# A hybrid block on one core: scans and branch operands spread over the rotations, operands behind copies, alternating halves, and the last residual in its PSUM bank

## The chip, the cores and the metric

One core of a Trainium2 chip. The time is device microseconds of one execution; before the change the median of three runs is 1061.51 us (1061.37 to 1062.74).

## The reference

One block of a network on 512 tokens behind 16 learned ones (T = 528), width 1024, all in fp32:

```python
z = rms_norm(h) @ w_in
u_rnn, u_gate, q, k, v, g_ret, ga, gb = split(z)
xr = causal_dwconv(u_rnn)                       # 4 taps, 1280 channels
hr = rg_lru(xr)                                 # h_t = a_t h_{t-1} + b_t, 10 blocks of 128 channels
o_a = hr * gelu(u_gate)
q, k = rotary(q, pos), rotary(k, pos) * RET_DK ** -0.5     # 4 heads of 256
o_b = head_rms(retention(q, k, v)) * silu(g_ret)
h = h + (sigmoid(ga) * (o_a @ w_brnn) + sigmoid(gb) * (o_b @ w_bret)) @ w_out
gate, val = split(causal_dwconv(rms_norm(h) @ w_up))
h = h + (gelu(gate) * val) @ w_down
out = rms_norm(h)[:, N_META:]
```

In the scan a = exp(log_a) and b = sqrt(1 - a^2) * (i * x), with two gates r and i that are products of 128 x 128 blocks.

## The kernel before

**Products.** TensorE (PE) works in fp16 on numbers split into a high and a low part: `split` (L93) makes the high part on ScalarE (ACT, L94) and the low part on VectorE (DVE, L95). A product of two such numbers takes three matmuls (`SPLIT`). Weights come from memory in units of 1 MB at most, through SyncE's queue into three buffers (`raw`), and are split into tiles named `wt`, two for a unit, ten buffers in all. The function `tick` issues the next steps of this splitting between the products, as far ahead as the buffers go, and `get` issues what a product needs at once. For some units the weights are also added in pairs on DVE first (L262 to L264), which saves products later.

**`project` (L427 to L433)** computes one tile of 128 channels by all tokens: 8 blocks k of the input, three matmuls for each, for each of two halves of the tokens (264 to 266 columns), 48 matmuls. Half 0 goes into the first and half 1 into the second bank of a PSUM tile of two banks. Blocks k = 0 to 3 use the first `wt` tile of the unit and k = 4 to 7 the second. Half 0 is done in full before half 1 begins.

**The order of work.** Up to `order.close()` each engine works in the order in which the program is written. From there on a scheduler orders the instructions of each engine, by when their inputs can be there and by how long what follows them is. The stages are, with the time at which they run:

- To 80 us: ten blocks n of the recurrent branch. `conv_product` (L629) calls `project` (for n = 0 to 2 half of it is done earlier), `conv_taps` adds four taps, `rnn_gates` makes the two gates.
- 80 to 140 us: ten blocks of the gate branch (L729 to L742, `project` and a gelu). Between them the list `SPREAD` puts steps of the recurrence: tanh, exp, and `rnn_scan` (L676) for blocks 0 to 4 at n = 7 and for blocks 5 to 9 at n = 9. `rnn_scan` is a square root on ACT (L678), a product (L679) and the scan (L680) on DVE, the scan over 528 columns.
- 140 to 230 us: four heads, q and k of each: eight calls of `rotary` (L758), "rotations" below. A rotation runs two `project` products into two PSUM tiles `pp`, then on DVE two cosine products (L770), two sine products (L771) and two sums (L772), and splits the two results (`qk`). Both PSUM tiles are read by both output halves. Four such tiles exist, so a product of the rotation after next waits until the DVE has read a tile of this one. `branch_a` (L745) makes the first branch's operand `oa` for a block: a product with the gate (L747) and a split. Two blocks stand behind rotation 0, three behind rotation 1, two behind 2 and three behind 3.
- 230 to 520 us: scores and values, `retention_out`, and the gates of the retention and of the mix. These run as `fast_products` (L872), seven products of half the size of a tile's, with a PSUM bank `pa` that is used again and again: `keep` (L885 to L887) copies it out on ACT, into `kept` or `last`, with high priority, and the next product waits for the copy. `ob_forms` (L1073) makes the operands of the second branch, 32 splits named `ob` on either engine, and puts them in the list `pending`; `flush` (L1108) issues one of them. `behind_copy` (L287) makes what is issued under it follow the latest `keep` copy, but only while `gating` is set, and it is cleared before the mix.
- 520 to 1000 us: the second branch, the output product, the norm, the feed-forward part.
- The end: the last sixth of the down projection for half of the columns is done by `down_plain` (L1602), 12 matmuls for each of four tiles of 128 tokens. For each tile (L1695 to L1713) DVE adds the residual `hv` (L1702) into `hu`, ACT squares it with a sum (L1704), DVE multiplies with the final gain (L1705), ACT takes the root (L1707), DVE inverts it (L1709) and scales the first 512 columns (L1710), which SyncE stores (L1711), and ACT scales the other 512 (L1712), which are stored on SyncE's or, for the last tile, on ACT's queue (L1713). `weigh` (L1673) has applied the gain to the columns that were ready before.

Of the kernel before, what the change touches and what calls it, by code (L numbers as in the profile page):

```python
# [8 lines left out]
F32 = mybir.dt.float32  # L9
# [5 lines left out]
P = 128  # L15
# [38 lines left out]
def hybrid_block_kernel(ctx, tc, x, meta, norm_mix_g, w_in, conv_w, conv_b, rg_a_w, rg_a_b,  # L54
# [372 lines left out]

    def project(ps, w, col, src, halves, nk):

        for hf, (c0, n) in enumerate(halves):  # L430
            for k in range(nk):
                for aw, ax in SPLIT:
                    nc.tensor.matmul(half_of(ps, halves, hf), w(aw, k, col, P), src(ax, k, c0, n),  # L433
                                     start=k == 0 and (aw, ax) == (0, 0), stop=k == nk - 1 and aw == 1)
# [197 lines left out]
    def conv_product(n):  # L632
        u, col = u_ur[n]
        if n in early:
            ps = early.pop(n)
            project_half(ps, get(u), col, xf, HR, 1)
        else:
            ps = acc("ps")
            project(ps, get(u), col, xf, HR, KD)
        return ps  # L640
# [28 lines left out]
    def rnn_decay(n):  # L669
# [4 lines left out]
        nc.vector.scalar_tensor_tensor(t, a2, 1.0, t, op0=ALU.add, op1=ALU.mult)  # L674

    def rnn_scan(n):  # L676
        r, t, xr = part(half_r, n), part(half_t, n), part(half_x, n)
        nc.scalar.activation(t, t, AF.Sqrt)  # L678
        nc.vector.tensor_mul(t, t, xr)  # L679
        nc.vector.tensor_tensor_scan(xr, r, t, 0.0, op0=ALU.mult, op1=ALU.add)  # L680
# [46 lines left out]
    ahead[0] = 6  # L727
    SPREAD = ((rnn_tanh, 2, 0), (rnn_decay, 3, 0), (rnn_tanh, 4, 5), (rnn_decay, 5, 5), (rnn_scan, 7, 0), (rnn_scan, 9, 5))
    for n in range(NR):  # L729
# [28 lines left out]
    def rotary(u, dst, halves, n, c0, s):  # L758
# [15 lines left out]
        for m in range(2):  # L774
            split(dst[m][:, 0, :n], dst[m][:, 1, :n], turned[m][:, :n], s)

    for h in range(HEADS):
        t = [[piece([P, 2, T], F16, f"qk{h}{i}{m}") for m in range(2)] for i in range(2)]
        qk.append(t)
        rotary(u_q[h], t[0], HQ, TQ, T0, S_QK / (SW * S_XN))  # L780
        if h < 2:
            for n in range(5 * h, 5 * h + 2):
                branch_a(n)
        rotary(u_k[h], t[1], HT, T, 0, S_QK / 16.0 / (SW * S_XN))
        if h < 2:
            for n in range(5 * h + 2, 5 * h + 5):
                branch_a(n)

# [319 lines left out]
    def flush(n=1):  # L1108

        for _ in range(min(n, len(pending))):  # L1110
            with behind_copy():
                pending.pop(0)()
# [488 lines left out]

    def down_plain(pc, tt):  # L1602

        w = wviews[u_dn[11]]
        n = 0
        for half in range(2):
            for b in range(2):
                t, c0 = acts[10 + b]["A%d%d" % (tt // 2 + 1, half + 1)]
                for ax, aw in SPLIT:
                    nc.tensor.matmul(pc, t[:, ax, c0 + tt % 2 * P:c0 + tt % 2 * P + P], w(aw, 2 * half + b, 0, 512),  # L1610
                                     start=n == 0, stop=n == 11)
                    n += 1
# [54 lines left out]
    for tt in range(4):  # L1667
# [3 lines left out]
                             AF.Square, accum_out=sums[:, tt, 0:1])  # L1671

    def weigh(tt, c0):  # L1673
        v = h2[tt].rearrange("p (a b) -> p a b", a=2)[:, :, c0:c0 + 256]
        nc.vector.tensor_tensor(v, v, gfin.rearrange("p (a b) -> p a b", a=2)[:, :, c0:c0 + 256], op=ALU.mult)

    for tt in range(4):
        weigh(tt, 0)
        nc.vector.tensor_scalar(sums[:, tt, 1:2], sums[:, tt, 0:1], inv_d, EPS, op0=ALU.mult, op1=ALU.add)


# [13 lines left out]
    for nm, tt in (("spare", 2), ("P1", 3), ("P6", 0), ("P7", 1)):  # L1695
        down_plain(pd[nm], tt)
        pv = pd[nm].rearrange("p (a b) -> p a b", a=2)
        hv = h2[tt].rearrange("p (a b) -> p a b", a=2)[:, :, 256:512]
        gv = gfin.rearrange("p (a b) -> p a b", a=2)[:, :, 256:512]
        hu = work.tile([P, 512], F32, name="hu", tag="w")  # L1700
        huv = hu.rearrange("p (a b) -> p a b", a=2)
        nc.vector.scalar_tensor_tensor(huv, pv, un, hv, op0=ALU.mult, op1=ALU.add)  # L1702
        junk = work.tile([P, 512], F32, name="junk", tag="w")
        nc.scalar.activation(junk, hu, AF.Square, accum_out=sums[:, tt, 2:3])  # L1704
        nc.vector.tensor_tensor(hv, huv, gv, op=ALU.mult)  # L1705
        sd = small.tile([P, 1], F32, name="sd")
        nc.scalar.activation(sd, sums[:, tt, 2:3], AF.Sqrt, scale=inv_d, bias=sums[:, tt, 1:2])  # L1707
        rs = small.tile([P, 1], F32, name="rs")
        nc.vector.reciprocal(rs, sd)  # L1709
        nc.vector.tensor_scalar_mul(h2[tt][:, 0:512], h2[tt][:, 0:512], rs)  # L1710
        nc.sync.dma_start(o2[tt * P:(tt + 1) * P, 0:512], h2[tt][:, 0:512])  # L1711
        nc.scalar.activation(h2[tt][:, 512:1024], h2[tt][:, 512:1024], AF.Copy, scale=rs)  # L1712
        (nc.scalar if tt == 1 else nc.sync).dma_start(o2[tt * P:(tt + 1) * P, 512:1024], h2[tt][:, 512:1024])  # L1713
    psum["scope"].close()
# [47 lines left out]
```

## Time and profile before

| | |
|---|---|
| median of 3 runs | 1061.51 us (1061.37 to 1062.74) |
| the profiled execution | 1061.5 us, its span 1059.8 us |
| busy in the span | PE 1039.7, DVE 872.8, ACT 594.0, weight load 865.9 us |
| granted TensorE clock | 0.999 |
| moved by DMA | 111.52 MB, of that 2.10 MB written |

The span is the time from the first to the last instruction or transfer that the profile shows; the execution's time has 1.7 us more. In a row of a timeline stand the start, the time taken, the engine, the line, the operation and its tiles (output <- input), and in brackets how long the engine was idle before it and which instruction it waited for. An engine's next instruction starts some 0.1 us before the end that a row shows, since instructions overlap in the engine's pipe: from start to start is the time that it takes up. "PE ps L433 <- DVE t L770" in a list of waits reads: the matmuls of L433 that write tile `ps` waited for the DVE instruction of L770 that writes `t`.

### The profile page before, as it was taken

The page shows a single profiled execution, that of the slowest core. Times are in us where ns is not written, and L with a number is a line of the kernel's source. Part 1 is how long each engine was busy: PE and PEld are TensorE (multiplying, and loading weights), DVE is VectorE, ACT ScalarE, POOL GpSimd, SP SyncE. Part 2 cuts the span into 40 slices and gives each one's busy share as a digit, 9 for nine tenths or more (in the row PEclk, how much of TensorE's full clock was granted, in tenths as well). Part 3 has the DMA queues.
Part 4 walks back from the last instruction along what each step waited for, and adds up shares of the span by engine and source line. Part 5 has one row for each costly group of instructions (what it writes and reads, how often), then busy time and mean ns, then how long its engine had stood idle before and what let it go on. Part 6 is the DMA issues. An engine that isn't in the chain of part 4 may idle for free.

```text
span 1059.8 us, 21437 instructions
## 1 busy us (share of the span) xinstructions
PE 1039.7 (98%) x9187; PEld 865.9 (82%) x9187; DVE 872.8 (82%) x1328; ACT 594.0 (56%) x941; POOL 6.9 (1%) x20
## 2 busy tenths in 40 slices
PE   9999999999999999999999999999999999999997
PEld 6888887875588888888888886588888888888885
DVE  6885699988669999996787885479989898988975
ACT  7568973434356768665454453375555455554442
POOL 2000000000000000000000000000000000000000
PEclk9999999999999999999999999999999999999999
DMA  9231243431012132344334356032423324214312
GB/s 295 97 127 58 81 140 120 159 123 40 1 41 93 68 105 66 107 114 128 108 113 129 98 219 194 1 116 85 160 87 113 120 81 136 65 61 139 101 41 80
DMA packets 109056, 111.52 MB, mean 105 GB/s; under 512 B 5675, under 2 KB 100625, under 8 KB 108961
## 3 DMA queue, kind: packets, MB, share of 16 engines
q1 hardware_dynamic: 108512, 109.74, 32.5%
q8 instruction: 72, 1.18, 0.5%
q10 hardware_dynamic: 160, 0.27, 0.1%
q0 software_dynamic: 288, 0.14, 0.1%
q14 instruction: 24, 0.19, 0.1%
HBM read 108.04 MB, written 2.10 MB: 104 GB/s over the span
## 4 chain that ended last, share of the span: by engine, by line
PE 72%; DVE 16%; ACT 9%; issue 2%; DMA 0%; ACTq 0%; DVEq 0%
PE ps L433 25%; PE P L1598 10%; PE pa L881 9%; DVE wt L95 5%; PE ps L1315 4%; PE pe L881 4%; PE pm L433 4%; PE ps L945 4%; ACT wt L94 2%; PE pb L881 2%; PE pa L1485 2%; PE ps L1035 2%; PE ps L447 2%; DVE rnn L680 1%; PE pa L969 1%
## 5 line engine op out<-in xcount | busy, mean ns | idle before, releaser
L433 PEld LDWEIGHTS <-wt 128*128 128x128 f16 x3840 | 372.5, 97 | 56.0 <-DVE t L770 2.6
L95 DVE SCALAR_TENSOR_TENSOR wt<-raw,wt 128x1024 f16<-128x1024 f32 (+2 forms) x286 | 310.0, 1100 | 57.1 <-ACT wt L94 56.2
L94 ACT ACTIVATE wt<-raw 128x1024 f16<-128x1024 f32 (+2 forms) x286 | 268.2, 958 | 118.7 <-PE P L1598 25.6
L881 PEld LDWEIGHTS <-wt 128*128 128x128 f16 x2016 | 195.2, 97 | 33.5 <-issue 6.7
L433 PE MATMUL ps<-x2h,wt 128*128 128x258 f16 (+1 forms) x1184 | 196.2, 272 | 0.0
L433 PE MATMUL ps<-xh,wt 128*128 128x258 f16 (+4 forms) x1056 | 179.0, 274 | 3.7 <-DVE t L770 2.9
L433 PE MATMUL ps<-x2l,wt 128*128 128x256 f16 (+1 forms) x592 | 160.9, 272 | 0.0
L433 PE MATMUL ps<-xl,wt 128*128 128x256 f16 (+4 forms) x528 | 144.5, 274 | 0.0
L1598 PE MATMUL P<-wt,act 128*128 128x256 f16 x792 | 88.3, 273 | 0.0
L1598 PEld LDWEIGHTS <-act 128*128 128x128 f16 x792 | 77.5, 98 | 9.0
L881 PE MATMUL pa<-xs,wt 128*128 128x258 f16 x576 | 71.3, 273 | 3.0 <-ACT kept L887 2.6
L1463 DVE SCALAR_TENSOR_TENSOR cv<-ps,vt,cv 128x512 f32<-128x512 f32 x80 | 59.3, 745 | 9.1 <-ACT cv L1461 8.5
L433 PE MATMUL pm<-oa,wt 128*128 128x256 f16 (+1 forms) x480 | 54.1, 273 | 0.0
L262 DVE TENSOR_TENSOR raw<-raw 128x1024 f32<-128x1024 f32 x43 | 52.4, 1219 | 0.7
L881 PE MATMUL pa<-ob,wt 128*128 128x257 f16 x384 | 45.7, 274 | 0.6 <-ACT last L887 0.5
L1315 PE MATMUL ps<-wt,mx 128*128 128x512 f16 x192 | 44.3, 378 | 0.0
L945 PE MATMUL ps<-wt,xh 128*128 128x512 f16 x128 | 38.3, 379 | 0.6 <-ACT qk L94 0.5
L1461 ACT ACTIVATE cv<-ps,vt,vt 128x512 f32<-128x512 f32 x40 | 30.5, 766 | 11.9 <-PE ps L433 11.9
L1485 PEld LDWEIGHTS <-wt 128*128 128x128 f16 x336 | 32.6, 97 | 4.4
L94 ACT ACTIVATE qk<-t 128x514 f16<-128x514 f32 (+1 forms) x16 | 10.2, 638 | 40.9 <-DVE t L772 40.9
L1315 PEld LDWEIGHTS <-mx 128*128 128x128 f16 x192 | 17.6, 98 | 18.5
L447 PEld LDWEIGHTS <-wt 128*128 128x128 f16 x288 | 27.9, 97 | 5.0 <-issue 0.6
(319 smaller groups left out, 1503.3 us busy)
## 6 DMA issues: line engine op xcount, KB each, us to landing
raw<-in_w_in SPq DMA_DIRECT2D x36, 1024.0 KB, 5.0
raw<-in_w_up SPq DMA_DIRECT2D x24, 1024.0 KB, 5.2
raw<-in_w_down SPq DMA_DIRECT2D x48, 256.0 KB, 3.4
raw<-in_w_branch_ret SPq DMA_DIRECT2D x16, 512.0 KB, 4.8
raw<-in_w_in SPq DMA_DIRECT2D x12, 512.0 KB, 4.6
raw<-in_w_branch_rnn SPq DMA_DIRECT2D x8, 640.0 KB, 4.7
raw<-in_w_out SPq DMA_DIRECT2D x4, 1024.0 KB, 5.0
xin<-in_x SPq DMA_DIRECT2D x4, 512.0 KB, 5.6
```

The costliest lines, as they stand in the source:

```text
L94: a = nc.scalar.activation(hi, src, AF.Copy, scale=s)
L95: b = nc.vector.scalar_tensor_tensor(lo, src, s, hi, op0=ALU.mult, op1=ALU.subtract)
L262: nc.vector.tensor_tensor(pair, pair, rv[:, :, right].rearrange("p (h k) c -> p h k c", h=2), op=ALU.add)
L433: nc.tensor.matmul(half_of(ps, halves, hf), w(aw, k, col, P), src(ax, k, c0, n), start=k == 0 and (aw, ax) == (0, 0), stop=k == nk - 1 and ...
L447: mm = nc.tensor.matmul(half_of(ps, halves, hf), w(aw, k, col, P), src(ax, k, c0, n), start=k == 0 and (aw, ax) == (0, 0), stop=k == KD - ...
L881: nc.tensor.matmul(ps[:, :n], ws[k // 4](wf, aw, k % 4), src(xf_, ax, k), start=first and k == 0 and (aw, ax) == (0, 0), stop=k == last_k ...
L945: nc.tensor.matmul(pb, xf(ax, k, XF + j0, nb), w(aw, k % 4, 0, 512), start=i == 0, stop=i == 23)
L1315: nc.tensor.matmul(ps[:, n], mx[k][:, a, c0:c0 + P], wo[k // 2](aw, k % 2, n * 512, 512), start=k == 0 and (a, aw) == (0, 0), stop=k == ks ...
L1461: nc.scalar.activation(vv_, taps[2], AF.Identity, scale=vt2[:, 96 + ch:97 + ch], bias=bias)
L1463: nc.vector.scalar_tensor_tensor(vv_, taps[j], vt2[:, 48 * j + ch:48 * j + ch + 1], vv_, op0=ALU.mult, op1=ALU.add)
L1485: nc.tensor.matmul(ps[:, :258], w(wf, aw, k), x2_form(xf_, ax, k), start=first and k == 0 and (aw, ax) == (0, 0), stop=k == 3 and aw == 1, ...
L1598: nc.tensor.matmul(pd[:, 256 * tt:256 * tt + 256], t[:, ax, c0 + tt * P:c0 + tt * P + P], w(wf, aw, i), start=q % 6 == 0 and tt == 0 and i ...
```

## The change

There are four edits. Line numbers behind the first edit move on by 1 to 24: in the rows below, L680 becomes L683, L770 to L772 become L773 to L775, L747 becomes L750, L887 becomes L892 and L920 becomes L925.

1. `project` gets `turns`: for the blocks n < 6 that run it whole (3, 4 and 5), both halves take their turn for each k and each of the three matmuls.
2. The square root is split off from `rnn_scan` and stays where both stood (`rnn_root`). The scans of blocks 5 to 9 go behind rotations 0 to 4, one each. The branch operands of blocks 0 to 4 go behind rotations 0 to 4, one each, and the others behind rotations 5 (two), 6 (two) and 7 (one).
3. `flush` puts the splits of the second branch's operands behind the latest `keep` copy always, and no longer only while `gating` is set.
4. For the last tile ACT writes the residual, scaled, into the PSUM bank ahead of the matmuls, and `down_plain` adds onto it. The square is taken from the bank, the scale and the gain are applied by one DVE instruction, and the two stores take columns 256 to 511 and 0 to 255 of both halves, one on SyncE's and one on ACT's queue, in runs of 1 KB where they were 2 KB. `weigh` becomes an instruction with a scale, and a small one adjusts the sum.

```diff
-    def project(ps, w, col, src, halves, nk):
-
-        for hf, (c0, n) in enumerate(halves):
-            for k in range(nk):
-                for aw, ax in SPLIT:
+    def project(ps, w, col, src, halves, nk, turns=False):
+
+        both = [0, 1]
+        for hfs in [both] if turns else [[0], [1]]:
+            for k, (aw, ax), hf in [(k, s, hf) for k in range(nk) for s in SPLIT for hf in hfs]:
+                    c0, n = halves[hf]
...
-            project(ps, get(u), col, xf, HR, KD)
+            project(ps, get(u), col, xf, HR, KD, n < 6)
...
+    def rnn_root(n):
+        nc.scalar.activation(half_t[n], half_t[n], AF.Sqrt)
+
     def rnn_scan(n):
         r, t, xr = part(half_r, n), part(half_t, n), part(half_x, n)
-        nc.scalar.activation(t, t, AF.Sqrt)
...
-    SPREAD = ((rnn_tanh, 2, 0), (rnn_decay, 3, 0), (rnn_tanh, 4, 5), (rnn_decay, 5, 5), (rnn_scan, 7, 0), (rnn_scan, 9, 5))
+    SPREAD = ((rnn_tanh, 2, 0), (rnn_decay, 3, 0), (rnn_tanh, 4, 5), (rnn_decay, 5, 5), (rnn_root, 7, 0), (rnn_scan, 7, 0), (rnn_root, 9, 5))
...
+    def between(i):
+        if i < 5:
+            rnn_scan(5 + i)
+        for n in ((i,), (5, 6), (7, 8), (9,))[max(0, i - 4)]:
+            branch_a(n)
+
...
         rotary(u_q[h], t[0], HQ, TQ, T0, S_QK / (SW * S_XN))
-        if h < 2:
-            for n in range(5 * h, 5 * h + 2):
-                branch_a(n)
+        between(2 * h)
         rotary(u_k[h], t[1], HT, T, 0, S_QK / 16.0 / (SW * S_XN))
-        if h < 2:
-            for n in range(5 * h + 2, 5 * h + 5):
-                branch_a(n)
+        between(2 * h + 1)
...
-            with behind_copy():
+            with tc.issue_after(last_keep[0]):
                 pending.pop(0)()
...
     def weigh(tt, c0):
...
-        nc.vector.tensor_tensor(v, v, gfin.rearrange("p (a b) -> p a b", a=2)[:, :, c0:c0 + 256], op=ALU.mult)
+        nc.vector.scalar_tensor_tensor(v, v, 1.0 / un if tt == LAST else 1.0,
...
+        if tt == LAST:
+            nc.scalar.activation(pv, hv, AF.Copy, scale=1.0 / un)
+            down_plain(pd[nm], tt, True)
+            junk = work.tile([P, 512], F32, name="junk", tag="w")
+            nc.scalar.activation(junk, pd[nm], AF.Square, scale=un, accum_out=sums[:, tt, 2:3])
+            nc.scalar.activation(sd, sums[:, tt, 2:3], AF.Sqrt, scale=inv_d / (un * un), bias=sums[:, tt, 3:4])
+            nc.vector.reciprocal(rs, sd)
+            ob_ = o2[tt * P:(tt + 1) * P].rearrange("t (a b) -> t a b", a=2)
+            nc.vector.scalar_tensor_tensor(hv, pv, rs, gv, op0=ALU.mult, op1=ALU.mult)
+            nc.sync.dma_start(ob_[:, :, 256:512], hv)
+            nc.scalar.activation(hb[:, :, 0:256], hb[:, :, 0:256], AF.Copy, scale=rs)
+            nc.scalar.dma_start(ob_[:, :, 0:256], hb[:, :, 0:256])
+            break
```

What this does to the order. On DVE, around rotation 0 in the program before, the twelve rows up to the second cosine product (`rnn` are tiles of the recurrence, L679 and L680 its product and scan, `ps` the PSUM tiles, `t_1966` and `t_1971` the two results of the rotation):

```order
L680 SCALAR_TENSOR_TENSOR rnn<-rnn 128x528
L679 TENSOR_TENSOR rnn<-rnn 128x528
L95 SCALAR_TENSOR_TENSOR wt<-raw,wt 128x1024
L680 SCALAR_TENSOR_TENSOR rnn<-rnn 128x528
L679 TENSOR_TENSOR rnn<-rnn 128x528
L95 SCALAR_TENSOR_TENSOR wt<-raw,wt 128x1024
L680 SCALAR_TENSOR_TENSOR rnn<-rnn 128x528
L679 TENSOR_TENSOR rnn<-rnn 128x528
L771 TENSOR_TENSOR t_1967<-ps,rope_1853 128x514
L680 SCALAR_TENSOR_TENSOR rnn<-rnn 128x528
L772 TENSOR_TENSOR t_1966<-t_1966,t_1967 128x514
L770 TENSOR_TENSOR t_1971<-ps,rope_1852 128x514
```

The same place in the changed program (L683 is the scan, L682 its product, `t_1956` and `t_1961` the results):

```order
L95 SCALAR_TENSOR_TENSOR wt<-raw,wt 128x1024
L773 TENSOR_TENSOR t_1956<-ps,rope_1842 128x514
L683 SCALAR_TENSOR_TENSOR rnn<-rnn 128x528
L95 SCALAR_TENSOR_TENSOR wt<-raw,wt 128x1024
L682 TENSOR_TENSOR rnn<-rnn 128x528 x2
L683 SCALAR_TENSOR_TENSOR rnn<-rnn 128x528
L95 SCALAR_TENSOR_TENSOR wt<-raw,wt 128x1024 x2
L774 TENSOR_TENSOR t_1957<-ps,rope_1843 128x514
L773 TENSOR_TENSOR t_1961<-ps,rope_1842 128x514
```

Both programs have the same instructions up to the product of the fifth scan and the weight split behind it. From that split to the second cosine product stood 6 weight splits, 6 scans, 5 scan products, one cosine product, one sine product and one sum; now it is 8 weight splits, 3 scans, 3 scan products, one cosine and one sine product. Of the scans that stand now behind it, two come after rotation 0 and 1 and one after rotation 2.

On PE, in the product of block 4 of the convolution, the first rows of before (each matmul has its weight load in front):

```order
L433 MATMUL ps<-xh,wt 128x266
L433 LDWEIGHTS wt
L433 MATMUL ps<-xl,wt 128x266
L433 LDWEIGHTS wt
L433 MATMUL ps<-xh,wt 128x266
```

and of the changed program:

```order
L434 MATMUL ps<-xh,wt 128x266
L434 LDWEIGHTS wt
L434 MATMUL ps<-xh,wt 128x265
L434 LDWEIGHTS wt
L434 MATMUL ps<-xl,wt 128x266
L434 LDWEIGHTS wt
L434 MATMUL ps<-xl,wt 128x265
```

The two halves (266 and 265 columns) alternate; the number of matmuls and of weight loads is the same.

On ACT, in a gate product of the mix (`g_5557` and `g_5556` are the gate's results, `pa` PE's bank, `ob_5835` an operand of the second branch), before:

```order
L920 ACT_TABLE_LOAD
L920 ACTIVATE g_5557<-g_5557 128x257
L887 ACTIVATE kept<-pa 128x257
L920 ACTIVATE g_5557<-pa 128x257
L94 ACTIVATE wt<-raw 128x1024
L920 ACTIVATE g_5556<-g_5556 128x514
L94 ACTIVATE ob_5835<-or_5016 128x257
L887 ACTIVATE kept<-pa 128x257
L94 ACTIVATE ob<-or_5017 128x514
```

and in the changed program:

```order
L892 ACTIVATE kept<-pa 128x257
L925 ACT_TABLE_LOAD
L925 ACTIVATE g_5557<-g_5557 128x257
L925 ACTIVATE g_5557<-pa 128x257
L94 ACTIVATE wt<-raw 128x1024
L925 ACTIVATE g_5556<-g_5556 128x514
L892 ACTIVATE kept<-pa 128x257
L94 ACTIVATE ob_5835<-or_5016 128x257
L94 ACTIVATE ob<-or_5017 128x514
```

The first copy has moved ahead of the table load, the second ahead of the operand's split.

More of the change, by code (lines that the diff above doesn't have):

```diff
@@ L1600, in down_product, with down_plain @@
                                  stop=q % 6 == last and i == 1 and ax == 1, skip_group_check=True)
-    def down_plain(pc, tt):
+    def down_plain(pc, tt, seeded):
         w = wviews[u_dn[11]]
@@ L1610, in down_plain @@
                     nc.tensor.matmul(pc, t[:, ax, c0 + tt % 2 * P:c0 + tt % 2 * P + P], w(aw, 2 * half + b, 0, 512),
-                                     start=n == 0, stop=n == 11)
+                                     start=n == 0 and not seeded, stop=n == 11, skip_group_check=seeded)
                     n += 1
@@ L1671, in hybrid_block_kernel @@
                              AF.Square, accum_out=sums[:, tt, 0:1])
+    LAST = 1
     def weigh(tt, c0):
         v = h2[tt].rearrange("p (a b) -> p a b", a=2)[:, :, c0:c0 + 256]
-        nc.vector.tensor_tensor(v, v, gfin.rearrange("p (a b) -> p a b", a=2)[:, :, c0:c0 + 256], op=ALU.mult)
+        nc.vector.scalar_tensor_tensor(v, v, 1.0 / un if tt == LAST else 1.0,
+                                       gfin.rearrange("p (a b) -> p a b", a=2)[:, :, c0:c0 + 256],
+                                       op0=ALU.mult, op1=ALU.mult)
     for tt in range(4):
@@ L1679, in hybrid_block_kernel @@
         nc.vector.tensor_scalar(sums[:, tt, 1:2], sums[:, tt, 0:1], inv_d, EPS, op0=ALU.mult, op1=ALU.add)
+    nc.vector.tensor_scalar_mul(sums[:, LAST, 3:4], sums[:, LAST, 1:2], 1.0 / (un * un))
     pd = products()
@@ L1695, in hybrid_block_kernel @@
     for nm, tt in (("spare", 2), ("P1", 3), ("P6", 0), ("P7", 1)):
-        down_plain(pd[nm], tt)
         pv = pd[nm].rearrange("p (a b) -> p a b", a=2)
-        hv = h2[tt].rearrange("p (a b) -> p a b", a=2)[:, :, 256:512]
-        gv = gfin.rearrange("p (a b) -> p a b", a=2)[:, :, 256:512]
+        hb = h2[tt].rearrange("p (a b) -> p a b", a=2)
+        hv, gv = hb[:, :, 256:512], gfin.rearrange("p (a b) -> p a b", a=2)[:, :, 256:512]
+        sd = small.tile([P, 1], F32, name="sd")
+        rs = small.tile([P, 1], F32, name="rs")
+        if tt == LAST:
[11 more added lines that the diff above has]
+            break
+        down_plain(pd[nm], tt, False)
         hu = work.tile([P, 512], F32, name="hu", tag="w")
@@ L1705, in hybrid_block_kernel @@
         nc.vector.tensor_tensor(hv, huv, gv, op=ALU.mult)
-        sd = small.tile([P, 1], F32, name="sd")
         nc.scalar.activation(sd, sums[:, tt, 2:3], AF.Sqrt, scale=inv_d, bias=sums[:, tt, 1:2])
-        rs = small.tile([P, 1], F32, name="rs")
         nc.vector.reciprocal(rs, sd)
@@ L1712, in hybrid_block_kernel @@
         nc.scalar.activation(h2[tt][:, 512:1024], h2[tt][:, 512:1024], AF.Copy, scale=rs)
-        (nc.scalar if tt == 1 else nc.sync).dma_start(o2[tt * P:(tt + 1) * P, 512:1024], h2[tt][:, 512:1024])
+        nc.sync.dma_start(o2[tt * P:(tt + 1) * P, 512:1024], h2[tt][:, 512:1024])
     psum["scope"].close()
```

## The prediction

> **What bounds the kernel now.** I read the page's busy times first, then busy times by stretches of 20 us, then what TensorE (PE) waited for, then the timelines around each such wait.
>
> ```profile
> span 1059.8 us, 21437 instructions
> PE 1039.7 (98%) x9187; PEld 865.9 (82%) x9187; DVE 872.8 (82%) x1328; ACT 594.0 (56%) x941; POOL 6.9 (1%) x20
> ```
>
> PE is busy for all but 20.1 us of the span. The change removes no matmul, so everything it can win lies in those 20 us. In the stretches the second column is the length and the next four are PE, weight load, DVE and ACT:
>
> ```profile
> 140.00:160.00 20.00, 20.00 (x182) 17.38 (x180) 20.00 (x23) 11.70 (x15) 0.00 (x0) 1.00 0.37 116
> 160.00:180.00 20.00, 17.70 (x160) 15.20 (x158) 20.00 (x30) 8.95 (x13) 0.00 (x0) 1.00 0.29 96
> 180.00:200.00 20.00, 19.39 (x175) 16.68 (x173) 20.00 (x28) 6.45 (x11) 0.00 (x0) 1.00 0.52 167
> 220.00:240.00 20.00, 19.55 (x145) 13.27 (x143) 16.83 (x33) 6.75 (x13) 0.00 (x0) 1.00 0.32 108
> 440.00:460.00 20.00, 18.41 (x166) 16.00 (x165) 19.96 (x34) 13.66 (x22) 0.00 (x0) 1.00 0.40 122
> 1040.00:1060.00 20.00, 13.51 (x77) 7.25 (x75) 11.46 (x23) 6.74 (x16) 0.00 (x0) 0.92 0.28 106
> ```
>
> PE loses 2.3 us at 160, 0.6 at 180, 1.6 at 440 and 6.5 in the last stretch; where it loses, DVE is full, except at the end. The waits of PE (total, times, longest) name the same places:
>
> ```profile
> PE ps L433 <- DVE t L770: 2.9, 2, 2.3
> PE pa L881 <- ACT kept L887: 2.6, 4, 1.4
> PE ps L433 <- DVE wt L95: 0.8, 1, 0.8
> PE pe L881 <- DVE g L908: 0.7, 1, 0.7
> ```
>
> So four separate edits meet 2.9, 0.8, 3.3 us of stalls and the end. I cost them one by one against the profiled execution's 1061.5 us, which is the median of the runs shown (1061.51), so nothing is converted.
>
> **Edit 1, alternating halves (blocks 3 to 5 of the convolution products).** The chain of waits and the timelines around the stall of 0.8:
>
> ```profile
> 41.37 1.22 DVE L95 SCALAR_TENSOR_TENSOR wt<-raw,wt 128x1024 f16<-128x1024 f32 x1
> 41.54 0.27 PE L433 MATMUL ps<-xl,wt 128*128 128x266 f16 x1
> 42.65 0.40 PE L433 MATMUL ps<-xh,wt 128*128 128x266 f16 x2 [0.83 <-DVE wt L95]
> 42.65 38.81 PE ps L433 x340
> 39.34 0.72 PE L433 MATMUL ps<-xs,gw 128*128 128x264 f16 x5
> 81.48 0.70 ACT L662 ACTIVATE rnn<-ps,vt 128x528 f32<-128x528 f32 x1 [1.51 <-PE ps L433]
> ```
>
> The second weight tile of block 4 is finished on DVE at 41.37 + 1.22 = 42.59; PE has by then done the 12 matmuls of the first half that need only the first tile, and stands. 340 matmuls take 38.81 us, 0.114 each, while a lone one takes 0.27: a stall also drains the pipe and costs its gap plus 0.27 - 0.114 = 0.16. So it costs 0.83 + 0.16 = 0.99. With both halves in turns the first tile serves 24 matmuls, 12 x 0.114 = 1.37 more, so the second tile is asked for 1.37 later than now, and its wait of 0.99 is gone with 0.38 to spare. Does the switch of bank between neighbours cost? The five gate matmuls from 39.34 hold a switch of half and take (0.72 - 0.28) / 4 = 0.11 each, so I take 0. As many weight loads are issued as before. The gain lasts only if others follow: at 81.48 ACT still waits 1.51 us for PE, so ACT moves up with it. Edit 1: -1.0, bounds -1.0 to 0 (given back wherever DVE is full, below).
>
> **Edit 2, scans and branch operands spread over the rotations.** DVE's timeline from the last common instruction to the product PE waits for, PE at that place, and the loads on ACT:
>
> ```profile
> 143.41 1.22 DVE L95 SCALAR_TENSOR_TENSOR wt<-raw,wt 128x1024 f16<-128x1024 f32 x1
> 144.55 1.25 DVE L680 TENSOR_TENSOR_SCAN rnn<-rnn 128x528 f32<-128x528 f32 x1
> 145.72 2.33 DVE L95 SCALAR_TENSOR_TENSOR wt<-raw,wt 128x1024 f16<-128x1024 f32 x2
> 160.27 1.24 DVE L680 TENSOR_TENSOR_SCAN rnn<-rnn 128x528 f32<-128x528 f32 x1
> 161.43 0.66 DVE L772 TENSOR_TENSOR t<-t,t 128x514 f32<-128x514 f32 x1
> 162.02 0.68 DVE L770 TENSOR_TENSOR t<-ps,rope 128x514 f32<-128x514 f32 x1
> 162.75 0.28 PE L433 MATMUL ps<-xh,wt 128*128 128x256 f16 x1 [2.30 <-DVE t L770]
> 153.20 2.00 ACT L94 ACTIVATE wt<-raw 128x1024 f16<-128x1024 f32 x2 [5.48 <-DMA raw<-in_w_in]
> ```
>
> From start to start a weight split takes DVE 1.14 (143.41 to 144.55), a scan 1.17 (144.55 to 145.72), a plain product or subtraction about 0.60 (161.43 to 162.02). PE needs the second tile that rotation 0 holds; it is free when the rotation's second cosine product (162.02) has read it. Between 143.41 and that product stand now 6 splits, 6 scans, 5 scan products and 3 rotary instructions: 6.84 + 7.02 + 3.0 + 1.8 = 18.66, that is 162.07, against 162.02 in the trace. In the changed order 8 splits, 3 scans, 3 scan products and 2 rotary instructions stand there: 9.12 + 3.51 + 1.8 + 1.2 = 15.63. The product comes 3.03 earlier, at about 159.0, and ends at 159.7; PE wants it at 162.75 - 2.30 = 160.45. So the 2.30 goes, with 0.7 to spare, or a stall of 0.3 if edit 1 brings PE forward by 1.0 and DVE not at all. The two added splits are queue risk: their high halves come from ACT, which waits for a load until 153.20 and ends the first at 154.2; DVE reaches it after 6 splits, 3 scans, 3 products and one rotary instruction, at 143.41 + 12.75 = 156.2. It doesn't wait.
>
> What is late next? The removed scans come back behind later rotations. A rotation on DVE is 8 rotary instructions, two splits of a weight unit, one scan with its product and one branch operand (two instructions): 8 x 0.6 + 2.28 + 1.77 + 1.2 = 10.1 us. PE takes 96 x 0.11 = 10.6. It fits, narrowly; the work put off needs room after 220, where DVE is idle for 3.2 us of 20. The second stall of L770 (2.9 - 2.3 = 0.6) is of the same kind and I let it go too. With the two drains: 2.9 + 0.32 = 3.2. Edit 2: -3.2, which is all that the stalls hold; the other bound, -1.0, is the first rival's.
>
> **Edit 3, retention operands behind the copies.** ACT's timeline at two of the stalls:
>
> ```profile
> 453.64 0.42 ACT L920 ACTIVATE g<-g 128x257 f32<-128x257 f32 x1 [0.60 <-DVE g L908]
> 453.96 0.37 ACT L887 ACTIVATE kept<-pa 128x257 f32<-128x257 f32 x1
> 459.79 0.42 ACT L94 ACTIVATE ob<-or 128x257 f16<-128x257 f32 x1 [1.70 <-DVE or L1067]
> 460.11 0.37 ACT L887 ACTIVATE kept<-pa 128x257 f32<-128x257 f32 x1
> ```
>
> A kept copy frees PE's bank, and at 459.79 it stands in ACT's queue behind an operand split that itself waited 1.70 us for DVE. In the changed order this copy stands ahead of that split, and the one at 453.96 ahead of the table load and of the gate function that waited for DVE. Upper end: all 2.6 + 0.7 and five drains of 0.16, -4.1. But DVE is full there (19.96 of 20), so the next PE wait, for a weight split or a sum on DVE, is close behind every one of these. I take a fifth, -0.9, nearest to the row of DVE's load; lower end +1.0, the split (1.14) that a moved operand can push behind a product. The scheduler also orders a few scores and values differently at 230 to 270, where PE loses 0.45 (220 to 240); I take -0.3 there, -0.5 to +0.3.
>
> **Edit 4, the last tile's end.** ACT, DVE and both store queues at the end:
>
> ```profile
> 1053.27 0.72 ACT L1712 ACTIVATE h<-h,rs 128x512 f32<-128x512 f32 x1 [0.23 <-DVE rs L1709]
> 1053.67 0.68 DVE L1702 SCALAR_TENSOR_TENSOR hu<-P,h 128x512 f32<-128x512 f32 x1
> 1054.39 0.63 ACT L1704 ACTIVATE junk<-hu 128x512 f32<-128x512 f32 x1 [0.40 <-DVE hu L1702]
> 1055.67 0.72 ACT L1712 ACTIVATE h<-h,rs 128x512 f32<-128x512 f32 x1 [0.23 <-DVE rs L1709]
> 1056.19 0.33 SPq L1711 DMA_DIRECT2D out<-h  x1
> 1056.42 0.38 ACTq L1713 DMA_DIRECT2D out<-h  x1
> out<-h SPq DMA_DIRECT2D x7, 256.0 KB, 2.2
> out<-h ACTq DMA_DIRECT2D x1, 256.0 KB, 2.5
> raw<-in_w_down SPq DMA_DIRECT2D x48, 256.0 KB, 3.4
> ```
>
> The residual sum hu leaves the chain, since its value is already in the bank; the square then waits for ACT's scaling of the tile before, to 1053.27 + 0.65 = 1053.92 instead of 1054.39. The chain behind it keeps its length, so it wins 0.47. Against that, both stores now start together, and each moves 1 KB runs where it moved 2 KB. The last store is 2.5 us on its way; the nearest row with 1 KB runs, the w_down loads of the same 256 KB, has 3.4. By the first the edit gives -0.47, by the second +0.43. I take -0.3: the loads queue behind one another and the last stores don't. [...] Seeding the bank is one more ACT copy (0.4 to 0.7) in a stretch where ACT is busy for a third; `weigh` keeps its length.
>
> **Sum.** -1.0 - 3.2 - 0.9 - 0.3 - 0.3 = -5.7: 1061.5 - 5.7 = 1055.8.
>
> **The rivals.** (a) *The stall moves on.* DVE is full from 140 to 200 and has the same work after as before; if PE, 3 us earlier, runs into the same queue one or two rotations later, edit 2 keeps only 1 of its 3.2 and edit 1 is given back whole, since PE waits for DVE. Then -1.0 - 0.9 - 0.6 = -2.5: 1059.0. For it: a margin of 0.5 us a rotation. Against it: what was moved is asked for only after the rotations. (b) *Edit 3 opens fully.* If DVE keeps up at 420 to 460, the 4.1 comes in place of 0.9: 1052.6. Against it: 19.96 of 20 us busy. (c) *Slower: a burst of operands ahead of a weight split.* Each flush now waits for the latest copy, so splits held back run together on DVE, up to four of 0.66 = 2.6 us, ahead of the low split of the weights that the next product reads. One such place costs 2.6, and it must happen three times (7.9) with edit 3's gain gone to end slower: 1061.5 - 4.8 + 7.9 = 1064.6. Against it: PE waits in that part for ACT's copies 2.6 us and never for an operand. (d) *The copies don't move PE.* If at edit 3's places the later sum is what PE needs, edit 3 is 0 and edit 2 as forecast: 1056.7, within my case's range.
>
> **How the numbers follow.** My case (with d) 0.69: with half of edit 3's upper end and the good ends of the others, -1.0 - 3.2 - 2.0 - 0.5 - 0.5 = -7.2, it reaches to 1054.3; with edit 1 given back, edit 3 at 0 and edit 4 at +0.4, -2.8, to 1058.7. (a) 0.17, (b) 0.08, (c) 0.04, and 0.02 for no change at all. The range runs from 1053.7 to 1059.4: my case and most of (a), leaving out (b), (c), no change and the tail of (a), some 0.2. About 0.2%, 2.1 us, is what a measurement of this kernel can tell from no change: faster means below 1059.4. My case and (b) and two thirds of (a) give 0.88 faster; a third of (a), no change and a mild (c) 0.09 same; (c) 0.03 slower.
>
> **What would show it.** Right: no PE wait on the 2.9 row and none at 42.65; the second cosine product of rotation 0 starting near 159 (less what edit 1 gives); no copy of `kept` behind an `ob` split, with some of its 2.6 back as a wait on `wt` or `g`; the last stores issued near 0.5 us earlier against PE's last matmul, landing 2.5 to 3 later. Wrong: a wait on the rotary products in a later rotation of over 1 us, or more PE idle time between 440 and 460 than the 1.6 us of now.

## The result, and the profile after

The changed kernel takes 1058.57 us (median of 7 runs) against 1062.3 for the kernel before, run beside it: a ratio of 0.9967, 95% interval 0.9957 to 0.9977. One run of 1346 us, with a mean granted clock of 0.752, is left out of that; the other six lie between 1058.34 and 1058.75. By the medians it is 3.7 us faster, by the spans of the two profiled executions (1059.8 and 1056.8) 3.0. The forecast was 5.7.

The page after the change, its first rows and the waits of PE (total, times, longest):

```profile
span 1056.8 us, 21446 instructions
PE 1038.8 (98%) x9187; PEld 866.2 (82%) x9187; DVE 872.0 (83%) x1327; ACT 594.3 (56%) x942; POOL 6.9 (1%) x20
```

```profile
PE ps L434 <- DVE t L773: 1.6, 2, 1.0
PE pa L886 <- ACT kept L892: 1.5, 2, 1.0
...
PE pe L886 <- DVE g L913: 1.0, 1, 1.0
```

The wait for the weight split at 42.65 is gone (it was 0.8). The wait for the cosine products, 2.9, is not gone but 1.6, and it has moved: the first of its two places was rotation 0, now they are rotations 1 and 2. The waits for kept copies fell from 2.6 to 1.5, and the one for the sum `g` grew from 0.7 to 1.0. DVE around those rotations, and then PE at the two waits:

```profile
158.03 0.69 DVE L773 TENSOR_TENSOR t<-ps,rope 128x514 f32<-128x514 f32 x1
...
169.89 0.70 DVE L773 TENSOR_TENSOR t<-ps,rope 128x528 f32<-128x528 f32 x1
...
177.06 1.25 DVE L683 TENSOR_TENSOR_SCAN rnn<-rnn 128x528 f32<-128x528 f32 x1
178.23 3.09 DVE L750 TENSOR_TENSOR rnn<-rnn 128x514 f32<-128x514 f32 x5
181.24 0.69 DVE L774 TENSOR_TENSOR t<-ps,rope 128x514 f32<-128x514 f32 x1
181.84 0.68 DVE L773 TENSOR_TENSOR t<-ps,rope 128x514 f32<-128x514 f32 x1
```

```profile
170.64 0.29 PE L434 MATMUL ps<-xh,wt 128*128 128x264 f16 x1 [0.60 <-DVE t L773]
...
182.67 0.27 PE L434 MATMUL ps<-xh,wt 128*128 128x256 f16 x1 [1.00 <-DVE t L773]
```

Rotation 0's second cosine product starts at 158.03: the 159.0 of the forecast, less the 1.0 by which edit 1 moved everything. From there to rotation 1's it is 11.86 us on DVE and from that to rotation 2's 11.95, while PE takes 10.6 for a rotation by the forecast's price, and ran for 11.0 between its two waits (182.67 - 1.00 - 170.64). Ahead of the last one the scheduler has put five branch products in a row (178.23).

At the end, PE's last matmuls in the profile of before and of after, and the last two stores after:

```profile
1052.05 1.46 PE L1610 MATMUL P<-wt,act 128*128 128x512 f16 x6
```

```profile
1048.80 1.46 PE L1615 MATMUL P<-wt,act 128*128 128x512 f16 x6
...
1052.66 0.64 SPq L1720 DMA_DIRECT2D out<-h  x1
```

```profile
1052.63 0.64 ACTq L1722 DMA_DIRECT2D out<-h  x1
```

PE ended at 1053.51 and ends at 1050.26 now, 3.25 earlier. From there to the end of the span it was 6.29 and is 6.54, so the end gave 0.25 back. The store on ACT's queue, the last one before, starts 0.54 earlier against PE's end (2.37 behind it, 2.91 before), but takes 0.64 to issue where it took 0.38. The store on SyncE's queue (first line) and it (second line) are 3.3 and 2.5 us on their way, against 2.0 and 2.5 before:

```profile
DMA to landing us min/median/max: 3.3/3.3/3.3
```

```profile
DMA to landing us min/median/max: 2.5/2.5/2.5
```

So the ledger between the profiles is: edit 1 -1.0, edit 2 -1.3 (2.9 us of waits become 1.6, in two places as before), edit 3 -1.0 (2.73 us of waits between 420 and 480 become 2.02, in two places fewer, each with a drain of an estimated 0.16), edit 4 +0.25. Together that is -3.05, where the spans differ by 3.0.

### The profile page after: what moved, and what is told of

Read it like the earlier page. It is cut to its first block, busy times and chain, and to the rows that moved or that the text cites. A ratio compares the mean times of both kernels' runs of the same rounds, so it can differ in the third digit from the quotient of the medians.

```text
span 1056.8 us, 21446 instructions
## 1 busy us (share of the span) xinstructions
PE 1038.8 (98%) x9187; PEld 866.2 (82%) x9187; DVE 872.0 (83%) x1327; ACT 594.3 (56%) x942; POOL 6.9 (1%) x20
## 4 chain that ended last, share of the span: by engine, by line
PE 74%; DVE 15%; ACT 8%; issue 2%; DMA 0%; ACTq 0%; DVEq 0%
PE ps L434 27%; PE P L1603 10%; PE pa L886 9%; DVE wt L95 4%; PE pe L886 4%; PE ps L1320 4%; PE pm L434 3%; PE ps L448 3%; PE pb L886 2%; PE ps L950 2%; PE pa L1490 2%; ACT wt L94 2%; PE ps L1040 2%; PE pa L974 1%; DVE raw L262 1%
## 5 line engine op out<-in xcount | busy, mean ns | idle before, releaser
L434 PE MATMUL ps<-xl,wt 128*128 128x256 f16 (+4 forms) x528 | 140.8, 274 | 0.0
L1466 ACT ACTIVATE cv<-ps,vt,vt 128x512 f32<-128x512 f32 x40 | 30.5, 766 | 11.9 <-PE ps L434 11.9
```

The costliest lines, as they stand in the source:

```text
L1466: nc.scalar.activation(vv_, taps[2], AF.Identity, scale=vt2[:, 96 + ch:97 + ch], bias=bias)
```

## The experiments

Each stands beside runs of the kernel before on the same chip:

| kernel | median us | before us | ratio, 95% interval |
|---|---|---|---|
| e1: edit 1 alone | 1061.52 | 1061.92 | 0.9994 (0.9985 to 1.0003) |
| e2: edit 2 alone | 1060.42 | 1061.92 | 0.9986 (0.9976 to 0.9995) |
| e3: edit 3 alone | 1060.93 | 1061.92 | 0.9994 (0.9985 to 1.0002) |
| e4: edit 4 alone | 1062.32 | 1061.92 | 1.0004 (0.9995 to 1.0012) |
| e5: changed, without edit 4 | 1058.28 | 1061.75 | 0.9963 (0.9951 to 0.9976) |
| e6: changed, last tile cut in two | 1057.76 | 1061.75 | 0.9958 (0.9944 to 0.9971) |
| e7: changed, operands held | 1061.12 | 1061.75 | 0.9993 (0.9984 to 1.0002) |
| e8: changed, scans and operands late | 1065.3 | 1061.75 | 1.0029 (1.0017 to 1.0041) |
| e9: e6, seven operands put off | 1059.8 | 1062.26 | 0.9979 (0.9970 to 0.9988) |
| e10: e6, five operands put off | 1057.03 | 1062.26 | 0.9952 (0.9940 to 0.9965) |
| e11: e10, put off further | 1060.95 | 1062.65 | 0.9983 (0.9974 to 0.9992) |
| e12: changed, scans back | 1059.54 | 1062.65 | 0.9977 (0.9968 to 0.9986) |

The times of the kernel before, and of some of the others, fall into two groups about 0.9 us apart (e1: 1060.66 to 1060.89 with a mean granted clock of 0.998 to 0.999, and 1061.52 to 1061.81 with 0.997); what makes them, as far as the runs show it, is told in the last section. The kernels were run in several rounds, and the kernel before is up to 0.3 apart between them (medians of its faster group from 1061.46 to 1061.75), so a difference of that size between rows of different rounds is not settled by the times alone. The changed kernel was not run again beside e5 to e12.

**The four edits one by one.** e1 has the new `project` and its call and nothing else of the diff; e2 the parts from `rnn_root` to `between`; e3 the line in `flush`; e4 everything from `down_plain` on.

```diff
...
-        for hf, (c0, n) in enumerate(halves):
...
+        for hfs in [both] if turns else [[0], [1]]:
...
```

> Edit 1 alone in the kernel before. Theory (the four edits add up): the wait on the weight split at 42.65 goes with its drain, PE runs 1.0 us ahead from there to the end: 1.0 us less, with the waits at 162 and 195 as long as before (2.3 and 0.6). Rival (DVE is full from 140 to 200 and sets the pace there): PE's lead is given back at the first rotary wait, which grows to 3.3, and the time is as before.

The waits in e1:

```profile
PE pa L882 <- ACT kept L888: 2.6, 4, 1.4
PE ps L434 <- DVE t L771: 2.4, 1, 2.4
```

The wait for the weight split is gone, and the one in rotation 0 is 2.4 instead of 2.3: DVE has moved forward with PE, since the chain at 81.48 led from PE to ACT and on. In each group of times e1 is 0.9 less than before (before 1061.6 to 1061.9 and 1062.2 to 1062.8). The theory held; the rival would have needed a wait of 3.3. The interval of the medians alone would not show it, since the two groups mix.

```diff
...
+        between(2 * h)
...
+        between(2 * h + 1)
```

> Edit 2 alone in the kernel before. Theory: the changed program's two new waits on the cosine products, in rotations 1 and 2 (0.6 and 1.0, with their drains 1.9), come from the order on DVE alone, above all from the five branch products in a row; they stand here too, and the time falls by 3.2 - 1.9 = 1.3. Rival: they come from edit 1, which brings PE forward by 1.0 while DVE is full; then they shrink to 0 and 0.2 here and the time falls by about 3.

In e2:

```profile
PE ps L433 <- DVE t L772: 1.6, 2, 1.0
...
PE ps L433 <- DVE wt L95: 0.8, 1, 0.8
```

The two new waits have the very length that they have beside the other edits, 1.6, so edit 1's lead doesn't make them. The span is 1.1 less than that of before, and the median 1.5 less, since e2 has only the faster group (1060.26 to 1060.64): besides the wait it takes away what follows on it.

```diff
-            with behind_copy():
+            with tc.issue_after(last_keep[0]):
```

> Edit 3 alone in the kernel before. Theory: between 400 and 480 PE loses 2.3 instead of 3.4, with two waits of about 1 us (a kept copy near 438, a sum on DVE near 452) in place of four: 1.0 less. Rival: the gain there needs PE's lead of 2.2 from the edits ahead of it; then nothing or less than 0.4.

The two waits that e3 has between 400 and 480:

```profile
440.88 1.48 PE L881 MATMUL pa<-xs,wt 128*128 128x258 f16 x12 [0.98 <-ACT kept L887]
...
455.26 0.27 PE L881 MATMUL pe<-xh,wt 128*128 128x258 f16 x1 [1.03 <-DVE g L908]
```

They are those of the changed kernel (0.98 and 1.04, there at 437.53 and 451.92), so this gain owes nothing to the others. Both lead to DVE: in the changed kernel the copy that PE waits for at 437.53 stands in ACT's queue behind a gate function that itself waited 1.85 us for a sum on DVE.

```profile
436.58 0.63 ACT L925 ACTIVATE g<-g 128x514 f32<-128x514 f32 x1 [1.85 <-DVE g L920]
437.12 0.37 ACT L892 ACTIVATE kept<-pa 128x257 f32<-128x257 f32 x1
```

In each group the times of e3 are 0.9 to 1.0 less than before (1060.70 to 1060.93, and 1061.46 to 1061.72 but for one of 1062.42).

```diff
...
+            nc.sync.dma_start(ob_[:, :, 256:512], hv)
+            nc.scalar.activation(hb[:, :, 0:256], hb[:, :, 0:256], AF.Copy, scale=rs)
+            nc.scalar.dma_start(ob_[:, :, 0:256], hb[:, :, 0:256])
...
```

> Edit 4 alone in the kernel before. Theory: the last stores are issued 0.3 to 0.5 earlier against PE's last matmul, but in 1 KB runs they take 3.3 us instead of 2.0 to 2.5: 0.3 slower. Rival: the stores take longer only because two start together, the chain's 0.5 is won: 0.3 less.

Slower by 0.4 in each group (1061.99 to 1062.33, 1062.66 to 1063.18). Its store on SyncE's queue takes 2.6 and the one on ACT's 3.3 us.

**The end.** e5 takes edit 4 back; e6 keeps the seeded bank and cuts the two scalings in halves:

```diff
-            nc.vector.scalar_tensor_tensor(hv, pv, rs, gv, op0=ALU.mult, op1=ALU.mult)
-            nc.sync.dma_start(ob_[:, :, 256:512], hv)
-            nc.scalar.activation(hb[:, :, 0:256], hb[:, :, 0:256], AF.Copy, scale=rs)
-            nc.scalar.dma_start(ob_[:, :, 0:256], hb[:, :, 0:256])
+            for a, q in ((0, nc.sync), (1, nc.scalar)):
+                nc.vector.scalar_tensor_tensor(hv[:, a], pv[:, a], rs, gv[:, a], op0=ALU.mult, op1=ALU.mult)
+                nc.scalar.activation(hb[:, a, 0:256], hb[:, a, 0:256], AF.Copy, scale=rs)
+                q.dma_start(ob_[:, a], hb[:, a])
```

> The changed kernel without edit 4. Theory (edit 4 costs 0.3 to 0.4 by its slower stores, and adds to the others): 1058.1, 0.4 less than the changed kernel. Rival (the tail's loss belongs to the kernel before alone): 1058.5, as changed.

> The changed kernel with the last tile's DVE and ACT instructions cut in two, so that each store takes 512 neighbouring columns, 2 KB runs as before, and the first store can start when half is done. Theory (the 1 KB runs cost what the shorter chain won): the first store is issued 0.3 earlier than in the changed kernel, the second at most 0.2 later, both take 2.0 to 2.5 instead of 3.3, and the time is 0.7 less than the changed kernel's, 1057.8. Rival (the two stores are slow because they share the transfer engines): they take 3 us and more here too, and the time is within 0.2 of 1058.5.

e5 is 0.3 less than the changed kernel, of the expected size, though their runs overlap (1058.22 to 1058.54 against 1058.34 to 1058.75); its profile agrees, with 6.26 us from PE's end to the end of the span against 6.54. e6 (1057.65 to 1057.93) is clear of both, 0.5 below e5, which ran beside it, and has 5.76 there. Its end:

```profile
1051.96 0.87 DVE L1720 SCALAR_TENSOR_TENSOR h<-P,rs,gfin 128x256 f32<-128x256 f32 x2
```

```profile
1052.50 0.33 SPq L1722 DMA_DIRECT2D out<-h  x1
```

```profile
1052.92 0.38 ACTq L1722 DMA_DIRECT2D out<-h  x1
```

```profile
DMA to landing us min/median/max: 2.0/2.1/2.3
```

The same bytes on the same two queues, 0.42 apart, in runs of 2 KB: 2.0 and 2.3 us on their way and 0.33 to 0.38 to issue, against 2.5 and 3.3, and 0.64, in runs of 1 KB. The rival's 3 us and more did not come. Two things differ, though, the length of the runs and that the stores start 0.42 apart instead of 0.03, and no run separates them: that it is the length is argued, not shown. What e6 does show is that the shorter chain is worth the 0.5 that the forecast gave it, once the stores are no slower than before.

**The rotations: order or sum?** e7 holds each branch operand behind the last split of its rotation, so that the five products can't gather; e8 holds scans and operands back to later rotations.

```diff
...
         for n in ((i,), (5, 6), (7, 8), (9,))[max(0, i - 4)]:
-            branch_a(n)
+            with tc.issue_after(turned_last[0]):
+                branch_a(n)
```

> The changed kernel with each branch operand held behind the last split of its rotation on DVE, so that the scheduler can't take five branch products in a row ahead of rotation 2's cosine product. Theory (the order is the cause of the two new waits): the wait of 1.0 in rotation 2 goes, the one of 0.6 in rotation 1 stays at 0 to 0.6, 1.2 to 1.9 less: about 1057. Rival (DVE is full from 140 to 200, what is taken from one rotation comes back in the next, or at the splits of q and k near 230): the waits move on and the time is within 0.4 of 1058.5.

```diff
...
-        if i < 5:
-            rnn_scan(5 + i)
-        for n in ((i,), (5, 6), (7, 8), (9,))[max(0, i - 4)]:
-            branch_a(n)
+        with tc.issue_after(turned_last[0]):
+            if 2 < i:
+                rnn_scan(2 + i)
+            for n in ((), (), (0,), (1,), (2, 3), (4, 5), (6, 7), (8, 9))[i]:
+                branch_a(n)
```

> The changed kernel with the five scans held behind rotations 3 to 7 and the ten branch operands behind rotations 2 to 7, on DVE. Theory (order): no wait on a rotary product after rotation 0, 1.7 to 1.9 less than the changed kernel, 1056.7; the work put off runs between 200 and 280, where DVE has some 8 us to spare. Rival (DVE's queue): the work put off meets the splits for the scores and PE waits there for 1 us or more, 1057.8 to 1058.5.

`turned_last[0]` is the last split of the rotation. In e7 (first fence) PE's longest wait is here, and in e8 (second) its two longest:

```profile
171.82 0.29 PE L434 MATMUL ps<-xh,wt 128*128 128x264 f16 x1 [1.67 <-DVE t L773]
```

```profile
229.62 0.90 PE L823 MATMUL ps<-qk,qk 128*128 128x144 f16 x6 [2.68 <-DVE t L773]
...
240.33 1.01 PE L953 MATMUL ps<-wt,xh 128*128 128x512 f16 x2 [2.97 <-DVE sf L830]
```

My theory fell, and so did the times that the rivals gave. In e7 the wait of rotation 2 goes, but that of rotation 1 grows from 0.60 to 1.67 and further ones come behind the last rotation: 2.5 slower than the changed kernel. In e8 there is no wait in any rotation, as I expected, and two large ones behind them: 6.7 slower. DVE's instructions up to the scores are the same in all of these kernels, and what is pushed out of one rotation is paid where PE next needs DVE. But the price is not the same: PE's waits between 140 and 260 come to 2.5 us in the changed kernel, 4.8 in e7 and 6.0 in e8. A held instruction can leave DVE without work. Of the 80 us from 140 to 220 DVE is busy for 78.95 in the changed kernel, 76.83 in e7 and 73.63 in e8. In e8 it lacks work above all at the start (window, length, then PE, weight load and DVE, which is busy for 17.10):

```profile
140.00:160.00 20.00, 20.00 (x181) 17.38 (x180) 17.10 (x19) 11.52 (x15) 0.00 (x0) 1.00 0.66 211
```

And of e8's 6.7 about half isn't waiting: PE's clock falls behind both waits (0.91 on average from 220 to 240, 0.92 from 240 to 260), an estimated 20 x 0.09 + 20 x 0.08 = 3.4 us. That DVE's idle time is what made the waits grow is read from these sums; no run separates it from the order.

So I let the work leave this stretch. e9 and e10 put operands off until behind the scores of heads 0 to 2, e11 until behind those of head 3. e10, as an edit of e6:

```diff
...
         if i < 5:
-            rnn_scan(5 + i)
-        for n in ((i,), (5, 6), (7, 8), (9,))[max(0, i - 4)]:
-            branch_a(n)
+            if i > 2:
+                with tc.issue_after(turned_last[0]):
+                    rnn_scan(5 + i)
+            else:
+                rnn_scan(5 + i)
+        if 1 < i < 7:
+            with tc.issue_after(turned_last[0]):
+                branch_a(i - 2)
...
     scores(2)
+    with tc.issue_after(scored[0]):
+        for n in range(5, NR):
+            branch_a(n)
```

> The kernel of the cut tail (1057.76), and with DVE relieved in the rotations: three branch operands behind rotations 1 to 3, the other seven behind the scores of heads 0 to 2 (near 290, where DVE is busy for 8 to 10 us of 20), and the last two scans held behind the splits of rotations 3 and 4. Theory (DVE's sum up to the scores is what bounds PE there): counted from the order with 1.14 for a weight split, 1.17 for a scan and 0.61 for the rest, each rotation's second cosine product is on time, the waits of 0.6 and 1.0 with their drains go, 1.9 less, and some of the 0.6 near 230: 1055.4 to 1055.9. Rival (the 8.4 us put off only stall the retention's start): a wait of 1 us or more appears between 280 and 330, 1056.9 or more.

> As the run before, with five operands behind rotations 2 to 6, held behind their splits, and five behind the scores. Theory (DVE's sum): by the same count all the rotations are on time, but DVE gets through the last one 2.4 later; the waits in the rotations go, those near 230 grow by 0 to 1: 1055.8 to 1056.8. Rival as above, with less put off: if the seven cost something near 290, the five cost less, and this kernel is the faster one.

> As e10, with the five operands put off further, behind the splits of head 3's scores (near 283), where DVE is busy for some 10 us of 20. Theory (an operand costs PE nothing where DVE has room ahead of the next instruction that PE needs): the waits of 0.4 and 0.8 near 271 and 277 go with their drains, none grows by more than 0.3 near 294: 1.0 to 1.3 less than e10, 1055.7 to 1056.0. Rival (6 us in a row hold up the head's norm, which PE waits for near 294): that wait of 0.2 grows by 1 or more, and the time is 1056.8 or more.

None of the three has a wait in the rotations. Where they wait instead, e9, e10 and e11:

```profile
273.49 1.00 PE L958 MATMUL ps<-wt,xh 128*128 128x512 f16 x2 [2.63 <-DVE v L95]
```

```profile
276.88 1.29 PE L829 MATMUL ps<-qk,qk 128*128 128x400 f16 x7 [0.76 <-DVE sf L836]
```

```profile
PE ps L1049 <- ACT ssum L1055: 3.0, 1, 3.0
```

In e9 the seven operands run from 262 to 272, not near 290 as I had expected, and hold up the split of the values: the rival was right about the cost, with 1059.8 where I had expected 1055.9 at most. In e10 five of them cost 0.76 and a smaller wait of 0.21, and 1057.03 us (1056.84 to 1057.12) is the best time of this study: 1.5 less than the changed kernel, and 0.9952 of the kernel before. It is 0.2 above the range that I expected. Of its gain over the changed kernel, e6's end has 0.8. e11 was to take away that 0.76 and made 3.0 of another kind, which ACT's rows show:

```profile
285.50 0.65 ACT L94 ACTIVATE sc<-sf 128x144 f16<-128x144 f32 x2 [0.28 <-DVE sf L836]
287.00 1.84 ACT L94 ACTIVATE oa<-rnn 128x514 f16<-128x514 f32 x3 [0.85 <-DVE rnn L750]
290.62 1.32 ACT L94 ACTIVATE oa<-rnn 128x514 f16<-128x514 f32 x2 [1.78 <-DVE rnn L750]
291.84 0.58 ACT L1053 ACTIVATE or<-ps 128x514 f32<-128x514 f32 x1
```

The operands' high halves stand in ACT's queue, wait there for products on DVE (0.85 and 1.78), and the two instructions that read PE's bank stand behind them, the copy of L1053 and the one of L1055 (at 292.32) that PE waited for. I had counted DVE's room only. The rival named the head's norm, which is where it waits, though not through DVE.

**Scans or operands?** e12 puts the scans back behind the square roots and leaves the operands spread.

```diff
-    SPREAD = ((rnn_tanh, 2, 0), (rnn_decay, 3, 0), (rnn_tanh, 4, 5), (rnn_decay, 5, 5), (rnn_root, 7, 0), (rnn_scan, 7, 0), (rnn_root, 9, 5))
+    SPREAD = ((rnn_tanh, 2, 0), (rnn_decay, 3, 0), (rnn_tanh, 4, 5), (rnn_decay, 5, 5), (rnn_root, 7, 0), (rnn_scan, 7, 0), (rnn_root, 9, 5), (rnn_scan, 9, 5))
...
-        if i < 5:
-            rnn_scan(5 + i)
```

> The changed kernel with its five scans back at one place, behind the square roots, and the operands still spread. Theory (by the count of DVE's rows): the wait on rotation 0's cosine product is back with 2.4, those of rotations 1 and 2 are gone: the scans were what made the 2.3 of before, the operands only the 0.6: 1058.5 + 2.5 - 1.9 = 1059.1, and runs in which TensorE's clock falls to a half behind that wait, as it did behind waits of 2.3 and more so far, take up to 1.7 longer; two groups of times. Rival (the spread operands matter most): the wait is under 1.5, the time under 1058.6, one group.

```profile
161.69 0.28 PE L434 MATMUL ps<-xh,wt 128*128 128x256 f16 x1 [2.33 <-DVE t L773]
```

The theory held: 2.33 in rotation 0, no wait in the later ones, and two groups of times, 1059.08 to 1059.54 and 1060.69 to 1060.95. The scans made the 2.3 of before; what made its 0.6 was not run by itself.

## Why the prediction was right and where it was not

The direction and the range were right (1058.57 in 1053.7 to 1059.4), the size was not: 3.7 instead of 5.7. The range held because it was drawn to take in most of rival (a), whose 1059.0 is nearer to the result than my 1055.8. Of the signs named for being right, the waits on the cosine products did not go (1.6 of 2.9 is left), and the longest of them, 1.00, stands just at the limit that I had named for being wrong.

- Edit 1, -1.0: right, 0.9 in e1. The second tile's wait went, the alternating matmuls start 0.115 us apart, against 0.114 without it (6 in 0.69 from 41.80 to 42.49 in the changed kernel's trace), and ACT and DVE followed.
- Edit 2, -3.2: the mechanism of rotation 0 was right to 0.1 us, the size was wrong. The step that failed is "what is late next": "10.1 us. PE takes 96 x 0.11 = 10.6. It fits, narrowly". I took one scan and one operand for a rotation, as the program is written. The rows that stand between the cosine products of rotations 0 and 1 are 2 scans, 2 weight splits and 12 others, 2.34 + 2.28 + 7.3 = 11.9, and between those of 1 and 2 they are 1 scan, 2 splits and 14 others, 1.17 + 2.28 + 8.5 = 11.95. Both sums could have been made from the order, as the one for rotation 0 was. PE asks 10.6 to 11.0 apart, so by them DVE falls behind by about 1.2 and then 0.9 us. The first eats up the 0.7 that rotation 0 had to spare and leaves 0.5, and the second comes whole: near the measured 0.60 and 1.00. Edit 2 is worth 1.3 between the profiles. Rival (a) had the mechanism (the stall moves on one and two rotations, into a full queue), but edit 1 was not given back with it, as (a) had it.
- Edit 3, -0.9: right, 1.0, and for the reason given, that DVE is full there: four waits between 420 and 480 (0.28, 0.33, 0.70, 1.42) became two, of 0.98 for a copy that DVE held up through ACT and of 1.04 for a sum on DVE. That a fifth of the upper end was the right share was a guess that came out.
- The scores and values at 230 to 270, -0.3: nothing, PE loses 0.47 from 240 to 260 after and 0.49 before.
- Edit 4, -0.3: wrong in sign, +0.3 to +0.4. The failed step is "the loads queue behind one another and the last stores don't". The 3.4 us of the nearest row with 1 KB runs was the better price: 3.3 was measured for the slower of the two. e6 agrees with it, with 2.0 and 2.3 us for the same stores in 2 KB runs, though it also starts them 0.42 apart.
- The profile of before was a cheap execution: PE's clock stayed whole behind its 2.30 us wait (1.00 from 160 to 180), which in other executions, to judge by their times and mean clocks (0.997 in the slower group beside e1, 0.999 in the profiled one), it didn't. Four of the seven runs of before beside the changed kernel are in the slower group (1062.3 to 1062.74), so their median is one of it. That adds to the medians' 3.7 what the profiles' 3.0 lacks, and it is luck, for the forecast had not counted it.

## What to carry to other kernels

Where an engine is full and another waits on it now and then, sum what stands in its queue between every two results that the other needs, not only ahead of the first, and take it from the order as scheduled, not as written. Moving work along within the full stretch moved the wait and kept 1.3 of 3.2 here, and holding work back made the waits longer (2.5 us in the changed kernel, 4.8 in e7, 6.0 in e8). e10 got rid of the waits in the stretch by taking half of the operands out of it; e11 shows that a place for them has to be free on every engine that they use. A chain shortened at the very end was worth its length where the last stores kept their 2 KB runs and started apart (0.5 us, e6), and less than nothing where they did neither (edit 4, +0.3 to +0.4).

## What the runs showed of the hardware

In seven profiles the clock granted to PE fell for a few us behind a wait of PE. In e1, behind the wait of 2.35 us at 162.06, three stretches from 162 to 170 (length, then busy time of each engine, then the granted clock):

```profile
162.00:163.00 1.00, 0.94 (x8) 0.80 (x9) 1.00 (x2) 0.06 (x1) 0.00 (x0) 0.86 0.00 0
163.00:166.40 3.40, 3.40 (x19) 2.37 (x18) 3.40 (x7) 2.56 (x5) 0.00 (x0) 0.54 0.02 5
166.40:170.00 3.60, 3.60 (x35) 3.16 (x33) 3.60 (x5) 1.01 (x2) 0.00 (x0) 1.00 0.00 0
```

19 matmuls in 3.4 us, where 33 would have run at the rate of the last row; in this trace the matmuls slow down about 0.6 us after PE resumes and are back at the old rate 3.5 us later. Behind the wait of 2.30 in the profile of before the clock did not fall (the 1.00 of 160 to 180). In the profiles with waits of 2.31 (e3), 2.32 (e4), 2.33 (e12), 2.63 (e9), 2.68 and 2.97 (e8) and 3.0 (e11) there is such a fall each time, with a mean of 0.91 or 0.92 over the 20 us stretch in which PE resumes, and in those whose longest wait behind the first 20 us is 1.67 or less (after, e2, e5, e6, e7, e10) there is none before the end of the kernel: 1.00 in every stretch up to 1040. No wait between 1.67 and 2.30 was profiled, and nothing here shows whether the length alone decides.

In e1 some 16 matmuls run 0.21 apart instead of 0.11, an estimated 1.6 us; of that the kernel before gets an estimated 0.8 back, since its next wait on DVE (0.6 and its drain) then goes, as in e1's list of waits: that fits the 0.9 between the two groups of times. In e12, which has no such next wait, the groups are 1.4 apart. The mean clocks fit too: 3.4 us at 0.54 lower the mean of 1060 us by 0.0015, and the groups of the kernel before show 0.998 to 1.0 and 0.997 in the runs beside e1. No kernel was profiled in both of its groups, so that the fall makes them is inferred from this. If it does, the wait of 2.3 us cost by this estimate up to 1.6 us more than itself in the executions with a fall, and taking it away gained more there than a profile without the fall shows.
